# Seven quarter products for the first feed-forward layer's gate and up tiles, in five parts

## The chip, the cores and the metric

The kernel runs on one core of a Trainium2 chip. The metric is the device time of one execution in microseconds; less is better. TensorE (PE) multiplies, VectorE (DVE), ScalarE (ACT) and GpSimd (POOL) work element by element, and SyncE (SP) issues all transfers from the chip's main memory.

## The reference

Two blocks of two layers each work on 512 tokens of 1024 values: attention mixers with a modulation in the first block, a state-space mixer and a convolution module in the second. A gated feed-forward layer follows each mixer, four in all, with 2816 hidden values:

```
def _swiglu(h, wg, wu, wd):
    return (jax.nn.silu(h @ wg) * (h @ wu)) @ wd
...
    cond = jax.nn.silu(c)
    for l in range(DEPTH):
        mod = cond @ ada_w[l] + ada_b[l]
        sh1, sc1, g1, sh2, sc2, g2 = [m[:, None, :] for m in jnp.split(mod, 6, axis=-1)]
...
        h = _rms_norm(x, norm_ffn[l]) * (1.0 + sc2) + sh2
        x = x + g2 * _swiglu(h, ffn_gate[l], ffn_up[l], ffn_down[l])
```

`mod` is a product of one vector with a 1024 x 6144 matrix for each layer of the first block: 48 columns of 128 values per layer.

## The kernel before

**Precision by splitting.** Each float32 operand becomes a high part `hi` (a rounded copy, made by ACT, L297) and a low part `lo` (the rest, made by DVE, L298); a product is three matmuls, hi by hi, hi by lo and lo by hi (`mm3`, L305 to L307). So every weight tile that lands in `raw` (three buffers) costs an ACT copy and a DVE subtraction before PE can use it. The split tiles have four buffers each.

**A feed-forward layer** (`ffn`) has 22 hidden tiles of 128 values. Its program alternates between *gate and up tiles* (`gu` or `gu7`, one per hidden tile, with result `d` as a hi and a lo part) and *down items* (`dn`, one per 128 output values, which multiply the `d` tiles of one part by `w_dn` and add into the stream `xT`, L675). `PARTS` says how many hidden tiles stand in a part.

- A **dense** tile (`gu`) needs 2 weight tiles x 8 row blocks x 3 = 48 matmuls of 512 columns, two splits on DVE, a product and the low part of `d`.
- A **seven** tile (`gu7`, `seven`) computes the same two products as a two by two block product from seven quarter products: 7 x 4 x 3 = 84 matmuls of 256 columns. DVE forms four sums of weights in `ws` (L710 to L714 here), splits three tiles of 1024 columns and one of 512, and joins the results (L740 and L816, L816 twice): 12 DVE instructions per tile in all with the low part of `d`. POOL adds two quarter results (L741). The sums of the activations (`crossed`, L687 to L693) are made once per layer.

Layer 0 (`ffn0`) computes all 22 tiles densely in three parts (`FIRST_S[0]` is 22); layers 1 to 3 compute 3, 2 and 2 tiles densely and the rest by seven products in four parts.

**The modulation stream.** Beside layer 0 runs `md.stream`: 56 columns of `ada` (8 of the first layer, 48 of the second) come in by transfers of 512 KB into `araw`, and each is reduced against `cb` by one DVE instruction of 1024 columns (L651, with an accumulator read), for a third of them followed by a small `gain` (L654). Two or three columns stand together, and `araw` has three buffers. `_weave` mixes the two streams by their costs in the order of the program text; a list scheduler then fixes the order on each engine. Every engine and SP's queue work strictly in that order, so an instruction that waits holds all behind it.

**Around layer 0.** The norm in front of it is made in halves of 256 tokens (`Split`): the first half of the dense tiles 0 and 1 runs while DVE builds the second half (L481, L492). The last two down items run as a `tail` in halves, so that the statistics of the next norm (`ss`, then `rb`) run under the second half's matmuls.

Of the kernel before, what the change touches and what calls it, by code (L numbers as in the profile page):

```python
# [10 lines left out]
F32 = mybir.dt.float32  # L11
F32R = mybir.dt.float32r
I32 = mybir.dt.int32
AF = mybir.ActivationFunctionType
OP = mybir.AluOpType
PSUM = bass.MemoryType.PSUM

T, NT, KC = 512, 4, 8
PARTS = ((0, 8), (8, 15), (15, 22))
PARTS_S = ((0, 6), (6, 12), (12, 17), (17, 22))  # L20
FIRST_S = (22, 3, 2, 2)
F_HID, FC = 2816, 22
NEG = -1e30

# [17 lines left out]
ROFF = {}  # L42
_o = 0
for _n, _w in ROW:
    ROFF[_n] = _o
    _o += _w
NROW = _o
CST = [("ident", 128), ("tri", 128), ("tri4", 128), ("cmask", 128), ("hones", 2)]
COFF = {}
_o = 0  # L50
# [40 lines left out]
def _layout(i):  # L91
# [20 lines left out]
    for n in range(4):  # L112
# [35 lines left out]
SSB = {"cbm": 2, "q": 16, "d": 14, "dt": 2, "xr": 1, "z": 2, "yg": 2, "xdt": 2, "L": 3, "xd": 1, "yo": 1, "sq": 1, "S": 1, "th": 1}  # L148
PHASES = {
# [9 lines left out]
    "ssm": (SSB,  # L159
# [63 lines left out]
def _program(nc, tc, a, out, stages=STAGES):  # L223
# [18 lines left out]
    def ptile(k, shape, dt, name):  # L242
        tag = ALIAS.get(name, name)
        _, p, bufs = cur[k]
        if k == "ps" and tag not in bufs:
            tag = {"tr": "pt", "st": "tr", "py": "tr"}[tag]
        return p.tile(shape, dt, tag=tag, name=name, bufs=bufs[tag])


# [1 line left out]

    xT = one.tile([128, KC, T], F32, name="xT")
    vec = one.tile([128, NVEC], F32, name="vec")
    row = one.tile([128, NROW], F32, name="row")
    cst = one.tile([128, NCST], F32, name="cst")
    ones = one.tile([128, 128], F32, name="ones")
    X = [xT[:, c] for c in range(KC)]
# [11 lines left out]
    def cs_(name, n):  # L269
        return cst[:, COFF[name]:COFF[name] + n]  # L270

    def rw(name, n):
        return row[:, ROFF[name]:ROFF[name] + n]

    ident = cs_("ident", 128)
    tri = cs_("tri", 128)
# [1 line left out]
    def tmp(name="t", dt=F32, n=T):  # L278
        return ptile("sb", [128, n], dt, name)
# [348 lines left out]
    class Mod:  # L628
# [25 lines left out]
                V.scalar_tensor_tensor(self.gain[:, o + c:o + c + 1], col, self.nb[:, o + c:o + c + 1],  # L654
                                       vc(nm, 8 * self.l + c), op0=OP.add, op1=OP.mult)

        def pair(self, j):
            for i in range(2):
                self.column(j, i)

        def stream(self, r):
            for j in r:
                self.pair(j)
                yield 1.0

        def col(self, o):
            return lambda c: self.mod[:, o + c:o + c + 1]
# [74 lines left out]
        return s, r1, bu[:, :hv]  # L742

    def ffn(n, nm, gcol, nxt):
        sparse = FIRST_S[n] < FC
        direct = isinstance(nm, Split)
        phase(("ffn1" if direct else "ffn") if sparse else "ffn0")
        x4 = []
        h = nm.h

# [14 lines left out]
        def gu(js):  # L765
            def it():
                gr = []
                for j in js:
                    with tc.issue_after(nm.mark.ins) if direct and j == 1 else nullcontext():
                        W = direct and j == 0 and nm.W or two(a[f"w_gu{n}"][j])  # L770
                        gr += [(psum("pg"), W[0]), (psum("pu"), W[1])]
                if js[0] == 0 and direct:
                    if sparse:
                        nm.keep = [tmp("z") for c in range(KC)]
                        for z, (hi, lo) in zip(nm.keep, h):
                            o = HALVES[0]
                            G.tensor_tensor(z[:, o], hi[:, o].bitcast(F32), lo[:, o].bitcast(F32), op=OP.add)
                    nm.lin([gr[:2], gr[2:]])
                else:
                    lin(gr, h)  # L780
                if sparse and len(x4) < 4:
                    sums(range(4) if direct else range(2 * js[0], 2 * js[0] + 2))
                if nm.R is None:
                    nm.finish().to_sbuf()
                R = nm.R
                for i, j in enumerate(js):
                    pg, pu = gr[2 * i][0], gr[2 * i + 1][0]
                    s = tmp("s")
                    if direct:
                        S.activation(s, pg, AF.Silu)  # L790
                        V.tensor_tensor(s, s, pu, op=OP.mult)
                    else:
                        u = tmp("su")
                        V.tensor_tensor(s, pg, R, op=OP.mult)
                        S.activation(s, s, AF.Silu)
                        V.tensor_tensor(u, pu, R, op=OP.mult)
                        V.tensor_tensor(s, s, u, op=OP.mult)
                    d[j] = hilo_of(s, to="d")
                return 10.4 * len(js), None
            return it  # L800
# [24 lines left out]
            return item(a[f"w_dn{n}"][m][:, lo:hi], lambda: [d[j] for j in range(lo, hi)], ev, hi - lo)  # L825

        items = []
        for lo, hi in (PARTS_S if sparse else PARTS):
            b = lo
            if lo == 0 and direct:  # L830
                items.append(gu([0, 1]))
                b = 2
            items += [gu([j]) if j < FIRST_S[n] else gu7(j) for j in range(b, hi)]
            at = TAIL_AT["final" if isinstance(nxt, Final) else 7]
            n_tail = at[0] if hi == FC and isinstance(nxt, Split) else 0
            items += [dn(m, lo, hi) for m in range(KC - n_tail)]
            if n_tail:
                items.append(tail(range(KC - n_tail, KC), lambda m: a[f"w_dn{n}"][m][:, lo:hi], hi - lo,
                                  lambda: [d[j] for j in range(lo, hi)], gcol, nxt, ("pj",) * n_tail, at[1:]))
# [132 lines left out]
    def mix0(make, following):  # L972
# [29 lines left out]
        for c in range(KC):  # L1002
# [9 lines left out]
                o = slice(j * 128, (j + 1) * 128)  # L1012
                mm3(pi[j], wh[:, 0, o], wl[:, 0, o], xh, xl, c == 0, c == KC - 1)
            mm3(pw[:72], wh[:, 0, 640:], wl[:, 0, 640:], xh, xl, c == 0, c == KC - 1)
        nc.sync.dma_start(row, a["row"].to_broadcast([128, NROW]))
        iq = {}
        B = {}
        for dst, key, i in ((iq, 4, 0), (B, 0, 1)):
# [16 lines left out]
        prod = small(64, "lp", bufs=1)  # L1035
        ls = small(2, "ls", bufs=1)
        for i in range(2):
            V.tensor_tensor_reduce(prod, rw(f"lam_q{i + 1}", 64), rw(f"lam_k{i + 1}", 64), 1.0, 0.0,
                                   OP.mult, OP.add, accum_out=ls[:, i:i + 1])
        with tc.issue_after(mk.ins):  # L1040
            S.activation(ls, ls, AF.Exp)
# [181 lines left out]
    def mix1(nm, md, nx):  # L1223
# [56 lines left out]
        def f3(u, pT):  # L1280
            i, t = u
            kv = ODD_Q[i] // 4
            p0 = 64 * (kv % 2)
            t0 = max(t - 1, 0)
            if t == 0:
                pys[i] = psum("py")
            o = slice(t * 64, t * 64 + 64)
            for s in range(t0, t + 1):
                c0 = s * 128 + p0
                E.matmul(pys[i][:, o], pT[:, (s - t0) * 128:(s - t0 + 1) * 128], Vn[kv // 2][:, c0:c0 + 64],  # L1290
                         start=(s == t0), stop=(s == t))
            if t == NT - 1:
                e = small(4, "es", bufs=2)
                S.activation(e, nms[i], AF.Exp, bias=row[:, ROFF["sinks"] + i:ROFF["sinks"] + i + 1])
                V.tensor_tensor(rs[i], rs[i], e, op=OP.add)
                head_out(i, pys.pop(i), rs[i], y, 0)

# [483 lines left out]
    if stages[0] != "mix0":  # L1781
        phase("ffn0")
        consts()
        nc.sync.dma_start(row, a["row"].to_broadcast([128, NROW]))
        if stages[0] in STAGES[:4]:
            cond()
            mods()
# [45 lines left out]
```

## Time and profile before

| what | value |
|---|---|
| time, median of 3 runs (lowest to highest) | 2675.92 us (2673.03 to 2680.61) |
| the profiled execution: its own time, its span | 2680.65 us, 2678.9 us |
| PE, DVE, ACT, POOL busy, share of the span | 94%, 73%, 47%, 21% |
| mean granted clock of PE | 0.972 |

Layer 0's products stand at about 373 to 744 us of the span, those of layer 1 at about 949 to 1316 us.

### The profile page before, as it was taken

The page shows a single profiled execution, that of the slowest core. Times are in us where ns is not written, and L with a number is a line of the kernel's source. Part 1 is how long each engine was busy: PE and PEld are TensorE (multiplying, and loading weights), DVE is VectorE, ACT ScalarE, POOL GpSimd, SP SyncE. Part 2 cuts the span into 40 slices and gives each one's busy share as a digit, 9 for nine tenths or more (in the row PEclk, how much of TensorE's full clock was granted, in tenths as well). Part 3 has the DMA queues.
Part 4 walks back from the last instruction along what each step waited for, and adds up shares of the span by engine and source line. Part 5 has one row for each costly group of instructions (what it writes and reads, how often), then busy time and mean ns, then how long its engine had stood idle before and what let it go on. Part 6 is the DMA issues. An engine that isn't in the chain of part 4 may idle for free.

```text
span 2678.9 us, 39465 instructions
## 1 busy us (share of the span) xinstructions
PE 2519.2 (94%) x15104; PEld 2222.2 (83%) x15104; DVE 1951.8 (73%) x3448; ACT 1255.4 (47%) x2291; POOL 557.1 (21%) x383
## 2 busy tenths in 40 slices
PE   5787989999999989999999999999999996999998
PEld 3666888888888879999788888789999786799997
DVE  7898755555456676677678887778777798678776
ACT  4456642222357543544455544454445554545443
POOL 3344220000112250000100000131012684321102
PEclk9889999999999999999999999999999997999999
DMA  7711025555421113333322121223333110132332
GB/s 259 240 56 40 32 87 204 173 176 193 149 73 40 40 56 102 95 104 104 103 79 72 45 89 56 87 81 103 108 104 106 69 63 16 64 117 94 102 98 87
DMA packets 84733, 265.75 MB, mean 99 GB/s; under 512 B 9280, under 2 KB 11712, under 8 KB 84544
## 3 DMA queue, kind: packets, MB, share of 16 engines
q1 hardware_dynamic: 84544, 263.24, 29.4%
q8 instruction: 118, 1.93, 0.3%
q14 instruction: 71, 0.58, 0.1%
HBM read 261.10 MB, written 2.10 MB: 98 GB/s over the span
## 4 chain that ended last, share of the span: by engine, by line
PE 71%; DVE 15%; issue 4%; POOL 3%; DMA 3%; ACT 3%; DVEq 0%; SPq 0%; POOLq 0%; ACTq 0%
PE pj L305 10%; PE pj L306 10%; PE pj L307 10%; PE pg L305 5%; PE pg L307 5%; PE pg L306 5%; PE pu L307 4%; PE pu L305 4%; PE pu L306 4%; DVE lo L298 3%; DMA raw<-w_gu 2%; POOL yp L1600 1%; PE pj L1412 1%; PE pj L1413 1%; PE pj L1414 1%
## 5 line engine op out<-in xcount | busy, mean ns | idle before, releaser
L297 ACT CAST hi<-raw 128x1024 fp32r<-128x1024 f32 (+5 forms) x445 | 393.5, 893 | 687.7 <-PE pj L306 265.9
L298 DVE TENSOR_TENSOR lo<-raw,hi 128x1024 fp32r<-128x1024 f32 (+5 forms) x435 | 465.7, 1073 | 170.7 <-ACT hi L297 167.9
L305 PE MATMUL pj<-d,hi 128*128 128x512 f32 (+1 forms) x940 | 353.3, 384 | 3.5 <-DVE xT L679 1.7
L306 PE MATMUL pj<-d,hi 128*128 128x512 f32 (+1 forms) x940 | 353.9, 379 | 0.0
L307 PE MATMUL pj<-d,lo 128*128 128x512 f32 (+1 forms) x940 | 351.0, 379 | 0.0
L741 POOL TENSOR_TENSOR bu<-bu 128x256 f32<-128x256 f32 x59 | 110.7, 1876 | 774.1 <-ACT bu L737 760.5
L305 PE MATMUL pu<-hi 128*128 128x256 f32 (+1 forms) x736 | 230.1, 314 | 3.2 <-DVE z L481 3.2
L307 PE MATMUL pu<-hi,lo 128*128 128x256 f32 (+1 forms) x736 | 231.1, 314 | 0.2 <-DVE lo L298 0.2
L306 PE MATMUL pu<-lo,hi 128*128 128x256 f32 (+1 forms) x736 | 229.8, 313 | 0.0
L305 PE MATMUL pj<-hi 128*128 128x512 f32 (+2 forms) x520 | 208.7, 405 | 3.9 <-ACT qk L901 1.2
L306 PE MATMUL pj<-lo,hi 128*128 128x512 f32 (+2 forms) x520 | 208.8, 402 | 3.6 <-DVE lo L492 2.4
L305 PEld LDWEIGHTS pj<-d,hi 128*128 128x128 f32 x940 | 177.2, 189 | 37.8 <-DVE xT L679 2.3
L307 PE MATMUL pj<-hi,lo 128*128 128x512 f32 (+2 forms) x520 | 206.5, 398 | 0.3 <-DVE lo L298 0.3
L306 PEld LDWEIGHTS pj<-d,hi 128*128 128x128 f32 x940 | 177.9, 189 | 33.2 <-issue 1.0
L307 PEld LDWEIGHTS pj<-d,lo 128*128 128x128 f32 x940 | 177.6, 189 | 33.3 <-issue 0.5
L305 PE MATMUL pg<-xh,hi 128*128 128x256 f32 x708 | 199.1, 281 | 1.2 <-ACT ua L734 1.1
L305 PE MATMUL pg<-hi 128*128 128x256 f32 (+1 forms) x572 | 192.2, 336 | 7.1 <-DVE z L481 4.5
L307 PE MATMUL pg<-xh,lo 128*128 128x256 f32 x708 | 198.1, 280 | 0.0
L306 PE MATMUL pg<-xl,hi 128*128 128x256 f32 x708 | 198.0, 280 | 0.0
L307 PE MATMUL pg<-hi,lo 128*128 128x256 f32 (+1 forms) x572 | 191.9, 335 | 4.6 <-DVE lo L298 4.5
L306 PE MATMUL pg<-lo,hi 128*128 128x256 f32 (+1 forms) x572 | 191.3, 335 | 0.6 <-DVE lo L492 0.6
L297 ACT CAST hi<-ws 128x1024 fp32r<-128x1024 f32 x118 | 123.5, 1049 | 116.3 <-DVE ws L711 50.7
(474 smaller groups left out, 6360.6 us busy)
## 6 DMA issues: line engine op xcount, KB each, us to landing
raw<-w_gu SPq DMA_DIRECT2D x176, 512.0 KB, 3.7
araw<-ada SPq DMA_DIRECT2D x96, 512.0 KB, 5.9
raw<-w_dn SPq DMA_DIRECT2D x48, 384.0 KB, 3.1
raw<-w_dn SPq DMA_DIRECT2D x48, 320.0 KB, 2.9
raw<-w_p SPq DMA_DIRECT2D x24, 512.0 KB, 3.6
raw<-w_out SPq DMA_DIRECT2D x32, 256.0 KB, 2.8
raw<-w_xs SPq DMA_DIRECT2D x16, 512.0 KB, 3.4
raw<-w_z SPq DMA_DIRECT2D x16, 512.0 KB, 3.4
```

The lines of the kernel that those rows point to most:

```text
L297: S.copy(hi, raw)
L298: (eng or V).tensor_tensor(lo, raw, hi.bitcast(F32), op=OP.subtract)
L305: E.matmul(ps, lh, rh, start=start, stop=False, **k)
L306: E.matmul(ps, lh, rl, start=False, stop=False, **k)
L307: E.matmul(ps, ll, rh, start=False, stop=stop, **k)
L741: G.tensor_tensor(bu[:, :hv], bu[:, :hv], bu[:, hv:], op=OP.add)
L1412: E.matmul(o, xh[:, ts], wh[:, k], start=st_, stop=False, skip_group_check=True)
L1413: E.matmul(o, xh[:, ts], wl[:, k], start=False, stop=False, skip_group_check=True)
L1414: E.matmul(o, xl[:, ts], wh[:, k], start=False, stop=sp, skip_group_check=True)
L1600: G.tensor_tensor(yp[:, sft:], yp[:, sft:], pr[:, sft:], op=OP.add)
```

## The change

Layer 0 takes the path of layer 1: tiles 0 to 2 stay dense, tiles 3 to 21 are made by seven products, and its parts are of 5, 5, 4, 4 and 4 tiles instead of 8, 7 and 7. Its buffers are set anew: `araw` two instead of three, `d` ten halves instead of sixteen, and the buffers of the seven products are added; squares share the tag `z`. The modulation stream is woven in by single columns instead of pairs. Four rows of constants that only the first mixer reads (`lam`) leave the lasting tile `row` for a tile of that stage, with a transfer of their own.

```diff
-PARTS = ((0, 8), (8, 15), (15, 22))
-PARTS_S = ((0, 6), (6, 12), (12, 17), (17, 22))
-FIRST_S = (22, 3, 2, 2)
+PARTS = (((0, 5), (5, 10), (10, 14), (14, 18), (18, 22)),) + (((0, 6), (6, 12), (12, 17), (17, 22)),) * 3
+FIRST_S = (3, 3, 2, 2)
...
-    "ffn0": ({"araw": 6, "cb": 2, "d": 16, "z": 3, "su": 2, "sq": 2}, {"mm": 6, "st": 1, "tr": 1}),
+    "ffn0": ({"araw": 4, "cb": 2, "d": 10, "z": 8, "ws": 3, "xh": 4, "xl": 4, "ua": 2, "bu": 2}, {"mm": 6, "st": 1, "tr": 1}),
...
-    row = one.tile([128, NROW], F32, name="row")
+    row = one.tile([128, NROW - NLAM], F32, name="row")
...
         def stream(self, r):
             for j in r:
-                self.pair(j)
-                yield 1.0
+                for i in range(2):
+                    self.column(j, i)
+                    yield 0.5
...
-        sparse = FIRST_S[n] < FC
         direct = isinstance(nm, Split)
-        phase(("ffn1" if direct else "ffn") if sparse else "ffn0")
+        phase("ffn" if n > 1 else f"ffn{n}")
...
-        for lo, hi in (PARTS_S if sparse else PARTS):
+        for lo, hi in PARTS[n]:
...
-        nc.sync.dma_start(row, a["row"].to_broadcast([128, NROW]))
+        rows()
+        lam = ptile("sb", [128, NLAM], F32, "lam")
+        nc.sync.dma_start(lam, a["row"][:, :NLAM].to_broadcast([128, NLAM]))
```

In the changed file lines stand about four further down (L298 is L302, L651 is L655, L675 is L676).

The first place is DVE's queue where layer 0 begins, behind the second half of the norm. Before, the columns of the stream (L651) stand there, then the splits of dense tile 2's two weights (L298):

```order
L651 ISA araw,mod_95<-araw,cb,vec 128x1024
L651 ISA mod_95 128x1
L492 SCALAR_TENSOR_TENSOR lo<-z,mod_95,hi 128x256
L651 ISA araw,mod_95<-araw,cb,vec 128x1024
L651 ISA mod_95 128x1
L651 ISA araw,mod_95<-araw,cb,vec 128x1024
L651 ISA mod_95 128x1
L651 ISA araw,mod_95<-araw,cb,vec 128x1024
L651 ISA mod_95 128x1
L298 TENSOR_TENSOR lo<-raw,hi 128x1024
```

Now four of the norm's low parts (L496) follow two columns, and the sums of the activations (L690, L691, L694) stand between the other columns, all ahead of the split of tile 2 (L302):

```order
L655 ISA araw,mod_95<-araw,cb,vec 128x1024
L655 ISA mod_95 128x1
L691 SCALAR_TENSOR_TENSOR ws<-ws,z 128x256 x2
L690 SCALAR_TENSOR_TENSOR ws<-z,ws 128x256
L655 ISA araw,mod_95<-araw,cb,vec 128x1024
L655 ISA mod_95 128x1
L691 SCALAR_TENSOR_TENSOR ws<-ws,z 128x256
L694 TENSOR_TENSOR xl<-ws,xh 128x1024
L655 ISA araw,mod_95<-araw,cb,vec 128x1024
L655 ISA mod_95 128x1
L302 TENSOR_TENSOR lo<-raw,hi 128x1024
```

So six columns stand ahead of tile 2's split as before, and seven instructions for the sums of the activations have come between.

The second place is DVE's queue in the middle of a run of gate and up tiles. Before, one dense tile there takes this much, two columns included:

```order
L298 TENSOR_TENSOR lo<-raw,hi 128x1024
L791 TENSOR_TENSOR s<-s,pu 128x512
L298 TENSOR_TENSOR lo<-raw,hi 128x1024
L390 TENSOR_TENSOR d<-s,d 128x512
L651 ISA araw,mod_100<-araw,cb,vec 128x1024
L651 ISA mod_100 128x1
L651 ISA araw,mod_100<-araw,cb,vec 128x1024
L651 ISA mod_100 128x1
```

Now most of a seven tile of the second part takes this much (from the third sum of weights `ws` on), one column and its `gain` (L658) included:

```order
L712 TENSOR_TENSOR ws<-ws,raw 128x512
L741 TENSOR_TENSOR s<-pu,ua 128x512
L655 ISA araw,mod_100<-araw,cb,vec 128x1024
L655 ISA mod_100 128x1
L658 SCALAR_TENSOR_TENSOR gain_101<-mod_100,nb_102,vec 128x1
L714 TENSOR_TENSOR ws<-ws,raw 128x512
L302 TENSOR_TENSOR lo<-ws,hi 128x1024
L815 SCALAR_TENSOR_TENSOR s<-s,bu 128x256
L815 SCALAR_TENSOR_TENSOR s<-s,pg 128x256
L302 TENSOR_TENSOR lo<-ws,hi 128x1024
L302 TENSOR_TENSOR lo<-raw,hi 128x512
L302 TENSOR_TENSOR lo<-raw,hi 128x1024
```

Two more sums (L711, L715) and the low part of `d` (L394) belong to a tile as well: four instructions of a dense tile have become twelve, and from tile to tile one or two columns stand between them.

The third place is SP's queue and DVE's where the second part goes over into its down items. SP issues, behind the last `w_gu` loads, those of `w_dn` two at a time with one column's transfer behind each pair, and goes on so to the end of the section:

```order
L709 DMA raw<-w_gu 128x1024 x2
L645 DMA araw<-ada 128x1024 x2
L295 DMA raw<-w_dn 128x640 x2
L645 DMA araw<-ada 128x1024
L295 DMA raw<-w_dn 128x640 x2
```

DVE takes two columns there, ahead of the low part of the part's last `d` (L394) and of the adds into `xT` (L676):

```order
L655 ISA araw,mod_100<-araw,cb,vec 128x1024
L655 ISA mod_100 128x1
L302 TENSOR_TENSOR lo<-raw,hi 128x640
L815 SCALAR_TENSOR_TENSOR s<-s,bu 128x256
L815 SCALAR_TENSOR_TENSOR s<-s,pg 128x256
L302 TENSOR_TENSOR lo<-raw,hi 128x640
L655 ISA araw,mod_100<-araw,cb,vec 128x1024
L655 ISA mod_100 128x1
L394 TENSOR_TENSOR d<-s,d 128x512
L676 SCALAR_TENSOR_TENSOR xT<-pj,mod_95,xT 128x512 x2
```

Before, pairs of columns stood behind such loads; now single ones do, and a load can be issued only when the DVE instruction that empties its buffer is done.

## Rows read from the trace of the kernel before

**Rows 1.** Windows: us, PE, PEld, DVE, ACT, POOL busy, clock, DMA, GB/s.

```profile
373.00:411.00 38.00, 35.70 (x236) 33.46 (x237) 28.99 (x53) 15.93 (x27) 5.49 (x6) 0.91 0.58 202
411.00:744.00 333.00, 331.52 (x1499) 274.89 (x1498) 178.02 (x257) 88.95 (x112) 9.67 (x8) 1.00 0.51 171
949.00:996.00 47.00, 40.19 (x273) 37.25 (x272) 42.47 (x62) 26.39 (x48) 29.26 (x28) 0.96 0.17 56
996.00:1316.00 320.00, 316.42 (x2134) 292.38 (x2133) 224.97 (x299) 149.23 (x238) 32.19 (x25) 0.99 0.32 102
```

**Rows 2.** ACT in order of time: first reads of dense and seven tiles' results.

```profile
637.53 0.59 ACT L790 ACTIVATE s<-pg 128x512 f32<-128x512 f32 x1
702.75 0.59 ACT L790 ACTIVATE s<-pg 128x512 f32<-128x512 f32 x1
...
1072.24 0.37 ACT L737 COPY bu<-pg 128x256 f32<-128x256 f32 x1
1092.22 0.37 ACT L737 COPY bu<-pg 128x256 f32<-128x256 f32 x1
```

**Rows 3.** Windows of four seven tiles of layer 1, their sum and mean.

```profile
sum 39.98, PE 39.98 PEld 39.94 DVE 34.01 ACT 24.18 POOL 4.50; mean PE 9.99 PEld 9.98 DVE 8.50 ACT 6.05 POOL 1.12
```

**Rows 4.** DVE's groups by form, 411 to 744 us: busy us, mean ns, idle before.

```profile
L651 DVE CUSTOM_DVE_ANT_0 araw<-araw,cb,vec 128x1024 f32<-128x1024 f32 x33 | 42.0, 1283 | 34.0 <-DMA araw<-ada 34.0
L651 DVE CUSTOM_DVE_ANT_0 araw<-araw,cb 128x1024 f32<-128x1024 f32 x16 | 19.6, 1225 | 49.9 <-DMA araw<-ada 49.8
L675 DVE SCALAR_TENSOR_TENSOR xT<-pj,mod,xT 128x512 f32<-128x512 f32 x22 | 16.5, 748 | 25.7 <-PE pj L307 25.7
L654 DVE SCALAR_TENSOR_TENSOR gain<-mod,nb,vec 128x1 f32<-128x1 f32 x16 | 3.5, 218 | 0.3
```

**Rows 5.** DVE's group that layer 1's stretch, 996 to 1316 us, holds for its successor.

```profile
L384 DVE SCALAR_TENSOR_TENSOR lo<-xT,vec,hi 128x512 fp32r<-128x512 f32 x8 | 9.2, 1181 | 0.2 <-ACT hi L383 0.2
```

**Rows 6.** DVE's waits, 411 to 744 us: us in total, times, longest.

```profile
DVE araw L651 <- DMA araw<-ada: 83.8, 24, 5.7
DVE lo L298 <- ACT hi L297: 38.6, 13, 7.3
```

**Rows 7.** DVE's waits in layer 1's steady stretch, 996 to 1316 us.

```profile
DVE lo L298 <- ACT hi L297: 35.2, 27, 4.7
DVE ws L710 <- DMA raw<-w_gu: 21.4, 14, 2.6
```

**Rows 8.** Landing of `araw` in 360 to 744 us, then of `w_gu` in 996 to 1316 us.

```profile
DMA to landing us min/median/max: 3.7/6.1/9.3
...
DMA to landing us min/median/max: 3.0/3.9/5.9
```

**Rows 9.** DVE in order of time where layer 0 begins.

```profile
390.11 1.75 DVE L651 CUSTOM_DVE_ANT_0 araw<-araw,cb,vec 128x1024 f32<-128x1024 f32 x1
391.80 0.08 DVE L651 DVE_READ_ACCUMULATOR2_ANT mod<- 128x1 f32 x1
...
397.42 1.29 DVE L651 CUSTOM_DVE_ANT_0 araw<-araw,cb,vec 128x1024 f32<-128x1024 f32 x1 [2.12 <-DMA araw<-ada]
...
399.89 1.22 DVE L298 TENSOR_TENSOR lo<-raw,hi 128x1024 fp32r<-128x1024 f32 x1
```

**Rows 10.** PE's wait for tile 2's split in layer 0's start.

```profile
PE pg L307 <- DVE lo L298: 1.9, 1, 1.9
```

**Rows 11.** DVE in order of time: a sum of activations in layer 1's start.

```profile
973.13 0.96 DVE L689 SCALAR_TENSOR_TENSOR ws<-z,ws 128x256 f32<-128x256 f32 x1
```

**Rows 12.** DVE and POOL groups by form, 1077.63 to 1107.99 us: joining a seven tile.

```profile
L741 POOL TENSOR_TENSOR bu<-bu 128x256 f32<-128x256 f32 x3 | 2.2, 742 | 25.0 <-ACT bu L737 25.0
...
L816 DVE SCALAR_TENSOR_TENSOR s<-s,bu 128x256 f32<-128x256 f32 x3 | 1.3, 417 | 0.0
```

**Rows 13.** The chain of waits at layer 0's end: start, us, what.

```profile
736.42 0.13 PE pj L307
...
738.49 0.61 PE ss L462 x4
...
742.61 0.43 PE rb L471 x2
```

More of the change, by code (lines that the diff above doesn't have):

```diff
@@ L47 @@
 NROW = _o
+NLAM = ROFF["sinks"]
 CST = [("ident", 128), ("tri", 128), ("tri4", 128), ("cmask", 128), ("hones", 2)]
@@ L244, in ptile @@
         _, p, bufs = cur[k]
-        if k == "ps" and tag not in bufs:
-            tag = {"tr": "pt", "st": "tr", "py": "tr"}[tag]
+        if tag not in bufs:
+            tag = {"tr": "pt", "st": "tr", "py": "tr", "sq": "z"}[tag]
         return p.tile(shape, dt, tag=tag, name=name, bufs=bufs[tag])
@@ L270, in cs_, with rw, rows @@
         return cst[:, COFF[name]:COFF[name] + n]
-    def rw(name, n):
-        return row[:, ROFF[name]:ROFF[name] + n]
+    def rw(name, n, o=0):
+        o += ROFF[name] - NLAM
+        return row[:, o:o + n]
+    def rows():
+        nc.sync.dma_start(row, a["row"][:, NLAM:].to_broadcast([128, NROW - NLAM]))
     ident = cs_("ident", 128)
@@ L655, in column @@
                                        vc(nm, 8 * self.l + c), op0=OP.add, op1=OP.mult)
-        def pair(self, j):
-            for i in range(2):
-                self.column(j, i)
         def stream(self, r):
             for j in r:
-                self.pair(j)
-                yield 1.0
+                for i in range(2):
+                    self.column(j, i)
+                    yield 0.5
         def col(self, o):
@@ L772, in it @@
                 if js[0] == 0 and direct:
[L773 to L777, printed above, removed]
+                    nm.keep = [tmp("z") for c in range(KC)]
+                    for z, (hi, lo) in zip(nm.keep, h):
+                        o = HALVES[0]
+                        G.tensor_tensor(z[:, o], hi[:, o].bitcast(F32), lo[:, o].bitcast(F32), op=OP.add)
                     nm.lin([gr[:2], gr[2:]])
@@ L780, in it @@
                     lin(gr, h)
-                if sparse and len(x4) < 4:
+                if len(x4) < 4:
                     sums(range(4) if direct else range(2 * js[0], 2 * js[0] + 2))
@@ L1037, in mix0 @@
         for i in range(2):
-            V.tensor_tensor_reduce(prod, rw(f"lam_q{i + 1}", 64), rw(f"lam_k{i + 1}", 64), 1.0, 0.0,
+            V.tensor_tensor_reduce(prod, lam[:, 128 * i:128 * i + 64], lam[:, 128 * i + 64:128 * i + 128], 1.0, 0.0,
                                    OP.mult, OP.add, accum_out=ls[:, i:i + 1])
@@ L1293, in f3 @@
                 e = small(4, "es", bufs=2)
-                S.activation(e, nms[i], AF.Exp, bias=row[:, ROFF["sinks"] + i:ROFF["sinks"] + i + 1])
+                S.activation(e, nms[i], AF.Exp, bias=rw("sinks", 1, i))
                 V.tensor_tensor(rs[i], rs[i], e, op=OP.add)
@@ L1783, in _program @@
         consts()
-        nc.sync.dma_start(row, a["row"].to_broadcast([128, NROW]))
+        rows()
         if stages[0] in STAGES[:4]:
```

2 rows, old and new, of the table PHASES are left out of this document.

## The prediction

> **What bounds the kernel now.** I read the windows by stage first. Between 411 and 744 us, layer 0's steady stretch from tile 3 on, PE is busy 331.5 of 333 us at full clock and DVE only 178 [rows 1]: the stage is bound by the number of matmul columns. DVE's waits there look large, 83.8 us for columns of the modulation and 38.6 us for ACT's high parts [rows 6], and cost nothing: DVE has far more time than work, and PE's busy time shows that no product waited for it. Layer 1 shows the form that layer 0 is to take. Its stretch from 996 to 1316 us does the same 19 hidden tiles with 320 us, PE 316 and DVE 225 [rows 1]. In the middle of its runs of gate and up tiles PE is busy all the time and DVE 8.50 of 9.99 us [rows 3]. So the seven products move a stage from "PE alone" to "PE, with DVE at 85%", and layer 1 has no modulation stream on DVE. The question is whether the columns still fit.
>
> **What the change saves on PE.** ACT's first reads of the results give the rhythm of the tiles: six dense tiles from 637.53 to 702.75, 10.87 us each; two seven tiles from 1072.24 to 1092.22, 9.99 us each [rows 2]. 0.88 us over 19 tiles is 16.7 us, if nothing else stops PE. The two stretches themselves differ by 333 - 320 = 13 us [rows 1]. Down items keep their number of columns; there are five sections of eight instead of three.
>
> **What it puts on DVE.** Layer 1's stretch holds 225 us of DVE work, of which 9.2 us belong to the layer after it [rows 5]: 215.8. The columns that now come beside it: 49 of them, 42.0 + 19.6 us, and 3.5 us for their gains [rows 4], 65.1 us. The fifth part means eight more adds into the stream than layer 1 has, at 0.75 us [rows 4], 6.0 us. Together 287 us. Against today's 333 us that leaves 46 us, against layer 1's 320 us 33 us. Work alone does not make DVE the bound; work and waits may. In a queue worked in order every wait is time that DVE does not get back unless PE has products in stock, and 33 us over 19 tiles is 1.7 us a tile.
>
> **What DVE will wait for.** A column can be taken when its 512 KB have landed, 6.1 us in the median after the issue, 3.7 at least [rows 8]; and it can be issued when the buffer is free and SP's queue has come to it. With two `araw` buffers a transfer is issued at the earliest when the column two before it is done. I went through the new order and added up, with the durations of these rows, the DVE work that stands between the instruction that releases the transfer and the column. In the runs of gate and up tiles it is 6 to 9 us: landing is covered. The loads of `w_gu` have 3.7 to 4.8 us of work against a landing of 3.9 [rows 8]: some 5 us of waits in all (layer 1 shows 21.4 us of them [rows 7], where DVE arrives early). In the down sections 15 columns have only 0.6 to 4.9 us, together 40.8, since each transfer stands in SP's queue behind two loads of `w_dn`, the second of which needs a buffer that a split has just emptied. The second column of the third place in the order shows it: the first split of 640 columns there empties the buffer, and up to the column stand two joins of 0.42 us [rows 12] and one split of 640 columns, less than the 1.22 of a whole one [rows 9]: under 2.1 us of work for a landing of some 5. Queued behind that column is the low part of the part's last `d`, which the down items need. At the median landing the 15 waits come to 15 x 6.1 - 40.8 = 51 us, at the shortest to 15 x 3.7 - 40.8 = 15. The loads of a down section are smaller than those of a gate and up run, which speaks for less than the median; I take the middle, 4.9 us, 33 us. DVE then needs 287 + 33 + 5 = 325 us for a stretch in which PE needs 316: DVE becomes the bound by a little, and the stretch takes 325 instead of 333, **-8 us**. The bounds: -16.7 (all waits fall where PE has products in stock), +10 (51 us of waits).
>
> **The start.** Six columns stand ahead of tile 2's split as before, and between them now seven instructions for the sums of the activations. Six of these cost 0.96 us beside POOL [rows 11] (0.42 where POOL is still [rows 12]) and one is as long as a split, 1.22 [rows 9]: 7.0 us. PE already waits 1.9 us for this split today [rows 10], so what makes it later lies on the path. Against it stands a wait of 2.12 us for a column [rows 9] that the sums fill: +4.9, I take **+5**. Bounds: +1.6 (sums at 0.42: 3.7 - 2.1); +13.1 (one whole landing of 6.1 more, since the third column has two buffers instead of three, and nothing is filled). Layer 1's start, which has these sums but no columns, is 47 us long against 38 here [rows 1]: 9 us more, between my value and the upper bound, but its lead-in differs, so I leave it as evidence for the bound.
>
> **The end.** The last two down items run in halves, so that the statistics `ss` pass under the second half; the first half's last product ends at 736.5, `ss` comes at 738.49 and `rb` at 742.61 [rows 13], 4.1 us of chain. With four `d` tiles in the last part instead of seven the second half has 2 x 3 x 3 matmuls fewer, at 0.13 us each [rows 13] 2.3 us of cover less. I take **+1.5** (0 to 2.3).
>
> **The rest.** The transfer of `lam` and the renamed buffers touch nothing that waits: 0. POOL's additions (19 of 0.742 us [rows 12]) are in layer 1's DVE time already; the columns that meet them are dearer: a column beside POOL took 1.75 us instead of 1.29 [rows 9]. An addition and a column together take 2.0 us, 19 times in 320 us: 12% or 6 of the 49 columns would meet one, at 0.46 us 2.7 us, which I leave inside the bounds of the waits. The Trainium skill, "SBUF — State Buffer", section "Who interferes with whom", says that DVE with two inputs in SBUF and GpSimd reading SBUF exclude each other for the whole instruction; the 1.75 us agrees with that. By it each POOL addition could hold DVE for its whole length, which is the third rival below.
>
> **Sum.** -8 + 5 + 1.5 = -1.5 us against the profiled execution's own 2680.65 us (span 2678.9, 1.75 around it). That execution is 4.7 us above the median; I put the difference on the median: 2675.92 - 1.5 = **2674.4 us**. A measurement of this kernel can tell 0.3%, 8 us, from no change.
>
> **Rivals.**
> - *DVE keeps pace, faster.* The scheduler lets matmuls of down items run between the products of the part's last tiles, so PE has work while DVE waits for a column, and DVE's waits of 122 us today [rows 6] cost PE nothing. Then the stretch gains the whole 16.7, the start costs 3, the end 1: 2663.2. Against it: every down item needs a split by DVE that stands behind the same columns, and DVE's stock of time is 33 us now, not 155. Chance 0.30.
> - *The column waits become the bound, slower.* Every one of the 15 columns in the down sections waits a median landing: 51 us, DVE 343, +10 + 5 + 1.5 = +16.5: 2692.4. It decides from 42.5 us of waits for columns on: DVE is then at 287 + 5 + 42.5 = 334.5, +1.5, and with 6.5 for start and end the loss is 8 us. For it: the landing of 6.1 us is that of today's stretch, at 171 GB/s [rows 1]; against it: the shorter loads. Chance 0.22.
> - *POOL holds DVE.* Were all 19 additions to hold a column for their whole 0.742 us, DVE has 325 + 14.1 = 339: +6 + 6.5 = +12.6, 2688.5. The one row that shows it cost 0.46, not 0.74, and the additions seldom meet a column. Chance 0.06.
>
> That the products are not removed at all cannot be: the order shows them gone.
>
> **From the cases to the numbers.** The forecast has 0.42 and a range of its own of 2665 to 2684 (landings from 4.3 to 5.5 us move the waits by 9). The first rival lies beyond -8 us, and so do some of the forecast's short landings: faster 0.33. The second and third lie beyond +8, and some of the forecast: slower 0.29; same 0.38. The range goes from a little below the first rival, 2660, to a little above the second, 2694.
>
> **What would show it.** In the windows of the new stretch (about 411 to 738): PE busy about 316 with some 9 us idle in four places, one at the head of each down section, and DVE above 280. DVE's waits for `araw` there near 33 us, nearly all in the down sections; under 20 speaks for the first rival, about 50 for the second. Tile 2's split done at about 406 instead of 401.1 [rows 9]. ACT's first reads 10 us apart in the middle of the runs; 10.9 would mean that DVE binds everywhere and that the sum of its work is wrong, not its waits. Between `ss` and `rb` PE idle by 1 to 2 us. The forecast falls if PE is idle mainly inside the runs of gate and up tiles, if the start loses over 10 us, or if the difference comes from another stage.

## The result, and the profile after

| | before | changed |
|---|---|---|
| median of 4 runs, us | 2678.27 | 2695.24 |
| lowest to highest | 2673.03 to 2681.32 | 2694.58 to 2700.74 |
| ratio, 95% interval | | 1.0077 (1.0061 to 1.0093) |
| span of the profiled execution | 2678.9 | 2692.8 |

The kernel is slower by 17 us between the medians, 0.77% by the ratio. The forecast of 2674.4 was wrong, and the result lies 1.2 us above its range. From the page of the changed kernel, how long each engine is busy (us, share of the span, number of instructions):

```profile
PE 2516.2 (93%) x15770; PEld 2245.8 (83%) x15770; DVE 2074.2 (77%) x3641; ACT 1315.9 (49%) x2428; POOL 601.1 (22%) x420
```

Four marks on PE divide layer 0: its second `rb` (382.6 us before, 375.2 now), the end of tile 2 before (413.5) and the first product with a sum of activations now (414.1), the first `ss` of the end (738.5, 750.8) and the last `rb` (757.7, 769.8). I call what lies between them start, stretch and end. The second mark is not quite the same place in the two kernels. In the changed one the last matmul of tile 2 (512 columns) begins at 411.16 and ends at 411.5, and matmuls of tile 3 (256 columns) follow:

```profile
411.16 0.39 PE L311 MATMUL pu<-hi,lo 128*128 128x512 f32 x1
411.38 0.28 PE L310 MATMUL pg<-lo,hi 128*128 128x256 f32 x1
```

So its start holds 2.6 us of tile 3's products. Windows of the kernel before for start and stretch (us; PE, PEld, DVE, ACT, POOL busy; granted clock; DMA share; GB/s):

```profile
382.60:413.50 30.90, 29.05 (x185) 26.35 (x184) 24.85 (x38) 13.92 (x23) 3.43 (x4) 0.94 0.62 221
413.50:738.50 325.00, 324.46 (x1453) 268.58 (x1452) 171.98 (x237) 86.70 (x108) 8.95 (x7) 1.00 0.51 172
```

The same of the changed kernel:

```profile
375.20:414.10 38.90, 33.80 (x206) 30.50 (x207) 38.36 (x50) 19.86 (x33) 19.33 (x14) 0.91 0.35 116
414.10:750.80 336.70, 316.81 (x2114) 291.16 (x2113) 278.07 (x418) 142.45 (x237) 32.06 (x26) 0.98 0.52 173
```

The start is 8.0 us longer (5.4 up to the end of tile 2), the stretch 11.7, the end as long as it was (19.0 against 19.2). In the profiled execution the program ahead of layer 0 was 7.4 us shorter and what follows 1.8 longer: 13.9 us in the span. How much of the 7.4 us is scatter is open: in the other profiles of kernels with the changed layout the second `rb` stands anywhere from 376.2 to 382.6. Layer 0 itself lost 19.5 us, between the 17 of the medians and the 20.6 of the ratio.

In the stretch PE is idle for 336.7 - 316.8 = 19.9 us, and before for 0.5. What it waits for, and what DVE waits for, from 411 to 744 us:

```profile
DVE araw L655 <- DMA araw<-ada: 23.3, 9, 5.0
DVE lo L302 <- ACT hi L301: 16.0, 20, 2.0
DVE xT L676 <- PE pj L311: 6.5, 4, 3.2
DVE ws L711 <- DMA raw<-w_gu: 3.6, 5, 2.0
...
PE pu L311 <- DVE lo L302: 11.1, 10, 1.9
```

DVE's waits for columns went from 83.8 us [rows 6] to 23.3, fewer than the 33 of the forecast; yet PE now waits for DVE. Windows of single sections show where: a run of five seven tiles (460 to 512), a down section (581 to 609) and a run of four tiles; behind them four short windows, to which I come below:

```profile
460.40:511.90 51.50, 46.82 (x386) 45.99 (x385) 50.42 (x77) 27.68 (x46) 4.42 (x4) 1.00 0.48 168
581.10:609.10 28.00, 26.80 (x135) 22.14 (x134) 18.77 (x31) 6.99 (x12) 0.87 (x1) 1.00 0.58 191
609.10:651.10 42.00, 39.12 (x302) 38.51 (x301) 38.93 (x61) 21.57 (x36) 3.34 (x3) 0.92 0.48 161
...
465.60:472.00 6.40, 6.37 (x53) 6.37 (x54) 5.96 (x8) 2.53 (x7) 0.00 (x0) 1.00 0.91 317
615.30:621.30 6.00, 5.97 (x28) 5.98 (x29) 5.71 (x8) 2.48 (x5) 0.00 (x0) 0.50 0.75 254
686.20:689.60 3.40, 3.40 (x18) 3.40 (x17) 3.40 (x5) 0.74 (x2) 0.00 (x0) 0.50 0.84 306
747.60:750.80 3.20, 2.68 (x12) 2.68 (x13) 0.86 (x4) 0.81 (x2) 1.46 (x2) 0.50 0.26 99
```

In the run of five DVE is busy 50.42 of 51.50 us, 98%, and in the run of four 38.93 of 42.00, 93%; in the down section 18.77 of 28.00, 67%. My 287 us of work against 333 was a mean over two regimes. ACT's first reads of the tiles' results show the rhythm of the tiles in these two runs:

```profile
471.86 0.38 ACT L738 COPY bu<-pg 128x256 f32<-128x256 f32 x1 [2.95 <-PE pg L311]
483.00 0.38 ACT L738 COPY bu<-pg 128x256 f32<-128x256 f32 x1 [2.96 <-PE pg L311]
492.98 0.38 ACT L738 COPY bu<-pg 128x256 f32<-128x256 f32 x1 [2.96 <-PE pg L311]
504.59 0.38 ACT L738 COPY bu<-pg 128x256 f32<-128x256 f32 x1 [2.95 <-PE pg L311]
...
623.98 0.38 ACT L738 COPY bu<-pg 128x256 f32<-128x256 f32 x1 [3.60 <-PE pg L311]
633.96 0.38 ACT L738 COPY bu<-pg 128x256 f32<-128x256 f32 x1 [2.96 <-PE pg L311]
643.95 0.38 ACT L738 COPY bu<-pg 128x256 f32<-128x256 f32 x1 [2.96 <-PE pg L311]
```

In the run of five the tiles come 11.1, 10.0 and 11.6 us apart; in the run of four 10.0, as in layer 1, and so in the runs on either side of it. There PE loses its time at the first tile of the run, just behind the down section, and at the last. Added up from PE's single waits, the 19.9 us of idle time are 7.5 at the first tiles of runs, 2.3 between tiles (in the run of five alone), 2.5 at last tiles, 3.1 in the down sections and 4.5 at the end.

The head of the run at 609 us shows how a first tile loses time, DVE in order of time, then PE's two waits:

```profile
609.04 1.23 DVE L655 CUSTOM_DVE_ANT_0 araw<-araw,cb 128x1024 f32<-128x1024 f32 x1
610.19 0.08 DVE L655 DVE_READ_ACCUMULATOR2_ANT mod<- 128x1 f32 x1
610.19 0.75 DVE L676 SCALAR_TENSOR_TENSOR xT<-pj,mod,xT 128x512 f32<-128x512 f32 x1
610.86 0.68 DVE L712 TENSOR_TENSOR ws<-ws,raw 128x512 f32<-128x512 f32 x1
611.45 1.28 DVE L655 CUSTOM_DVE_ANT_0 araw<-araw,cb,vec 128x1024 f32<-128x1024 f32 x1
...
614.05 1.22 DVE L302 TENSOR_TENSOR lo<-ws,hi 128x1024 fp32r<-128x1024 f32 x1
...
612.75 0.38 PE L309 MATMUL pu<-xh,hi 128*128 128x256 f32 x1 [0.65 <-ACT hi L301]
...
615.33 0.58 PE L311 MATMUL pu<-xh,lo 128*128 128x256 f32 x1 [1.80 <-DVE lo L302]
```

Two columns and the adds of the down section before stand in DVE's queue between the sums of weights of the first tile; the low part that PE needs comes out at 615.3, 1.80 us late. Behind that wait the granted clock is 0.50 from 615.3 to 621.3, the lower of the two levels (1.2 GHz), at which 28 matmuls of 256 columns take 6.0 us, 0.21 each, where the run goes at 9.99 / 84 = 0.12. So this wait of 1.8 us costs some 2.6 us more. Not every such wait does: the short windows above show the clock at 0.50 behind another wait of 1.80 us (at 684.7) from 686.2 to 689.6 and around one of 4.53 us (at 748.1), but at 1.00 behind one of 1.89 us (at 465.6).

### The profile page after: what moved, and what is told of

It is laid out like the page before. It is cut to its first block, busy times and chain, and to the rows that moved or that the text cites. A ratio compares the mean times of both kernels' runs of the same rounds, so it can differ in the third digit from the quotient of the medians.

```text
span 2692.8 us, 41333 instructions
## 1 busy us (share of the span) xinstructions
PE 2516.2 (93%) x15770; PEld 2245.8 (83%) x15770; DVE 2074.2 (77%) x3641; ACT 1315.9 (49%) x2428; POOL 601.1 (22%) x420
## 4 chain that ended last, share of the span: by engine, by line
PE 63%; DVE 20%; DMA 6%; issue 5%; ACT 3%; POOL 3%; SPq 0%; DVEq 0%; POOLq 0%; ACTq 0%
PE pj L309 9%; PE pj L310 8%; PE pj L311 8%; PE pg L311 4%; PE pg L309 4%; PE pg L310 4%; DVE lo L302 4%; DMA raw<-w_gu 4%; PE pu L311 3%; PE pu L310 3%; PE pu L309 3%; DMA araw<-ada 2%; DVE araw L655 2%; POOL yp L1601 2%; PE pj L1413 1%
## 5 line engine op out<-in xcount | busy, mean ns | idle before, releaser
L301 ACT CAST hi<-raw 128x1024 fp32r<-128x1024 f32 (+4 forms) x460 | 386.0, 852 | 543.7 <-PE pj L310 209.2
L302 DVE TENSOR_TENSOR lo<-raw,hi 128x1024 fp32r<-128x1024 f32 (+4 forms) x450 | 458.1, 1023 | 149.2 <-ACT hi L301 145.3
L742 POOL TENSOR_TENSOR bu<-bu 128x256 f32<-128x256 f32 x78 | 130.1, 1668 | 1070.3 <-ACT bu L738 1010.0
L309 PE MATMUL pg<-xh,hi 128*128 128x256 f32 x936 | 264.4, 282 | 2.1 <-ACT ua L735 1.1
L311 PE MATMUL pg<-xh,lo 128*128 128x256 f32 x936 | 262.7, 281 | 0.0
L310 PE MATMUL pg<-xl,hi 128*128 128x256 f32 x936 | 262.5, 280 | 0.0
L301 ACT CAST hi<-ws 128x1024 fp32r<-128x1024 f32 x156 | 163.3, 1049 | 143.8 <-DVE ws L712 71.6
L302 DVE TENSOR_TENSOR lo<-ws,hi 128x1024 fp32r<-128x1024 f32 x156 | 196.5, 1264 | 19.8 <-ACT hi L301 19.5
L311 PEld LDWEIGHTS pj<-d,lo 128*128 128x128 f32 x934 | 176.5, 189 | 35.4 <-DVE lo L302 3.0
L309 PEld LDWEIGHTS pg<-xh,hi 128*128 128x128 f32 x936 | 177.7, 190 | 5.0 <-ACT ua L735 1.9
L310 PEld LDWEIGHTS pg<-xl,hi 128*128 128x128 f32 x936 | 177.3, 189 | 1.5
```

Source lines behind the costliest of these rows:

```text
L301: S.copy(hi, raw)
L302: (eng or V).tensor_tensor(lo, raw, hi.bitcast(F32), op=OP.subtract)
L309: E.matmul(ps, lh, rh, start=start, stop=False, **k)
L310: E.matmul(ps, lh, rl, start=False, stop=False, **k)
L311: E.matmul(ps, ll, rh, start=False, stop=stop, **k)
L742: G.tensor_tensor(bu[:, :hv], bu[:, :hv], bu[:, hv:], op=OP.add)
```

## The experiments

What the kernels gave, from windows between the marks (the medians of the kernel before beside them were 2675.4 us for 1 to 4, 2677.1 for 5 to 8 and 2677.7 for 9 to 12; for the kernels with tile 3 dense, tile 2's end ends the start, which in the others would be 2.2 to 2.7 us shorter by that mark, 4.1 in the second; "idle" is the stretch less PE's busy time):

| kernel | median us, ratio to before (95%) | start | stretch | PE busy, idle in it |
|---|---|---|---|---|
| before | 2678.3 | 30.9 | 325.0 | 324.5, 0.5 |
| changed | 2695.2, 1.0077 | 38.9 | 336.7 | 316.8, 19.9 |
| 1 short reduction | 2686.5, 1.0044 (1.0028 to 1.0059) | 35.7 | 327.7 | 313.0, 14.7 |
| 2 short transfer | 2689.3, 1.0052 (1.0036 to 1.0068) | 35.4 | 330.1 | 315.3, 14.8 |
| 3 both short | 2676.4, 1.0008 (0.9992 to 1.0025) | 33.2 | 317.7 | 308.6, 9.1 |
| 4 columns to down items | 2698.0, 1.0093 (1.0068 to 1.0117) | 39.1 | 337.3 | 316.2, 21.1 |
| 5 dense, five parts | 2687.9, 1.0038 (1.0024 to 1.0053) | 37.8 | 331.9 | 327.9, 4.0 |
| 6 lam rows alone | 2679.9, 1.0010 (0.9998 to 1.0022) | | | |
| 7 columns on POOL | 2763.5, 1.0330 (1.0314 to 1.0345) | | | |
| 8 last eight tiles seven | 2693.6, 1.0058 (1.0040 to 1.0075) | 36.5 | 336.2 | 325.9, 10.3 |
| 9 fewer columns in the start | 2702.1, 1.0088 (1.0072 to 1.0104) | 34.1 | 345.6 | 319.5, 26.2 |
| 10 end mended | 2705.5, 1.0099 (1.0082 to 1.0115) | 39.1 | 342.9 | 319.4, 23.6 |
| 11 start and end | 2708.0, 1.0116 (1.0101 to 1.0131) | 33.9 | 349.8 | 321.7, 28.1 |
| 12 both mended, both short | 2669.4, 0.9962 (0.9951 to 0.9974) | 32.2 | 316.3 | 309.2, 7.1 |

**1 to 3: which cost of a column is it?** Theory A is DVE's work in the runs, theory B the waits for landing. `beside[0]` is set for the stream beside layer 0 alone. The first edit is that of the second and third kernel, the other that of the first and third; the second reduces seven copies of the 128 elements instead.

```diff
+            w = 128 if beside[0] else 1024
-            nc.sync.dma_start(r, a["ada"][self.l, j][:, i])
+            nc.sync.dma_start(r[:, :w], a["ada"][self.l, j][:, i][:, :w])
...
+                v = 128 if beside[0] else 1024
-                V.tensor_tensor_reduce(r, r, cbx[0], 1.0, 0.0 if gain else b, OP.mult, OP.add, accum_out=col)
+                V.tensor_tensor_reduce(r[:, :v], r[:, :v], cbx[0][:, :v], 1.0, 0.0 if gain else b, OP.mult, OP.add, accum_out=col)
```

> The columns beside layer 0 are reduced over 128 of their 1024 elements, so their values are not those of the reference; their transfers stay whole. DVE spends about 0.25 us on a column instead of 1.3, on 49 columns some 50 us less. Theory A, DVE's work in the runs of gate and up tiles is what binds (1.8 columns a tile on top of 8.5 us of a 9.99 us tile): the 12 us of PE's waits there and the 5 us of half clock behind them go, about 2680 us. Theory B, the waits for the landing of columns bind: the transfers are as before, so 2691 to 2699 us.

> The columns beside layer 0 come by transfers of 128 instead of 1024 elements per partition, and DVE reduces seven copies of these, 896 elements, so it works nearly as long as before (about 1.1 us) and the values are not those of the reference. Theory A: DVE's work is almost unchanged, so about 2690 us, at most 5 us below the changed kernel. Theory B: the 23 us of waits for araw go and with them most of the loss, 2675 to 2683 us.

> Both at once: transfers of 128 elements and reductions over 128, values not those of the reference. Both theories: the layer runs at PE's speed, stretch near 308 us instead of 337; what is left of the loss then comes from the start and the end: 2665 to 2672 us. Theory A sees the first experiment close to this one, theory B the second.

Neither theory holds alone: the first kernel's 2686.5 us lie between the two, the second's 2689.3 are theory A's, and the third's 2676.4 lie above what both gave. Against the changed kernel the stretch is 9.0 us shorter with short work, 6.6 with short transfers, 19.0 with both. That both give more than the two together (15.6) comes from one profile of each; by the ratios the gains are 8.8, 6.7 and 18.5 us, each uncertain by some 5 us, so it is not shown. The waits for columns of the first kernel, then of the second (411 to 744 us):

```profile
DVE araw L657 <- DMA araw<-ada: 39.1, 21, 5.1
```

```profile
DVE araw L659 <- DMA araw<-ada: 20.0, 11, 4.0
```

With 38 us less of work in that window (DVE is busy 238.93 us of it instead of 276.75) DVE, in the first kernel, waits 39.1 instead of 23.3 us for columns: it comes to them earlier and stands in its queue all the same, with the splits behind it. The two costs lie in one queue, and what the work gives up the waits partly take. In the second kernel the waits have hardly gone, though a transfer lands after 3.2 us in the median instead of 5.1. So it does not test theory B as it was meant to, and where its 6.6 us come from is open: DVE's waits for high parts fell from 16.0 to 12.0 us, and the traffic in the stretch from 173 to 109 GB/s. The third kernel shows what the seven products are worth, the stretch's window:

```profile
412.20:729.90 317.70, 308.58 (x2114) 285.44 (x2112) 235.30 (x419) 144.77 (x238) 31.54 (x26) 1.00 0.37 112
```

PE needs 308.6 us for the same 2114 matmuls at full clock, 15.9 less than before (about 1 us of it, an estimate, is work on the other side of a mark: 24 matmuls of 256 columns, 0.12 us each, stand in the start, and 18 of 512, 0.23 each, have come in from the end for 18 of 256). In the changed kernel they take 316.8, 8.2 us more. In its three places at 0.50 PE is busy 12.0 us, so 6.0 of these 8.2 us are lower clock; what the other 2.2 are is not shown.

**4: more columns with the down items.** A wrapper gives each item of layer 0 a cost of its own for the weave:

```diff
+        def cost(c, it):
+            def f():
+                k, post = it()
+                return (c if n == 0 else k), post
+            return f
...
-            items += [dn(m, lo, hi) for m in range(KC - n_tail)]
+            items += [cost(0.75, dn(m, lo, hi)) for m in range(KC - n_tail)]
```

(1.0 for a seven tile, 6 for tiles 0 to 2, 3 for the last four items, 56.5 in all instead of 345.)

> The weave's costs in layer 0 are set to 1.0 for a seven tile and 0.75 for a down item, so that about one column stands with each seven tile and three with each four down items. Theory A: DVE has 18.8 us of work in 28 us of a down section and 98 % in a gate and up run, so moving work there gains 8 to 15 us: 2680 to 2687 us. Theory B: more columns where the landing is not covered, so more waits: 2695 to 2705 us.

Nothing gained: 2698.0 us, in theory B's range, stretch 337.3. The loads are issued ahead of their use, so in DVE's order most of the moved columns stand ahead of the low part of a run's last `d`, and DVE waits 26.8 us for columns from 411 to 744 us instead of 23.3. The experiment did not bring columns into the idle time of the down sections, and so does not decide what that would give.

**5 and 6: the rest of the change without seven products.** The fifth sets `FIRST_S[0]` to 22 in the changed kernel (the sums of the activations are still formed in the start, without use); the sixth takes only the hunks on `lam` and `row` into the kernel before.

> The changed kernel with all 22 tiles of layer 0 dense again: five parts, two araw buffers, single columns and the moved lam rows stay. If the loss comes from the columns beside seven tiles, nothing is left of it: the stretch from the second rb to the first ss of the tail stays within 3 us of the 355.9 of the kernel before, and the time is 2668 to 2680 us. If the five parts, the two buffers or the single columns cost something by themselves, it shows here: above 2685 us. The first mixer ends some 4 to 8 us earlier than before if the lam rows do that.

> The kernel before with only the four lam rows moved to their own tile and transfer. If the earlier first rb of layer 0 (359 to 363 us in five profiles against 367 before) is this edit's, the time is 2668 to 2672 us and rb stands at 359 to 363; if it is the scatter of a profile or comes with the new layer 0, the time is 2673 to 2678 us.

The lam rows do nothing that can be measured: the first `rb` stands at 366.2 us, and the 2679.9 us lie above both of the ranges. But the dense kernel with five parts is slower by 0.38%, the second case of its expectation, which neither theory had. So about half of the loss of 0.77% is there without one seven product, and whether the parts, the buffers, the single columns or the sums in the start bring it, this kernel does not separate. Its start is 6.9 us longer than before, its stretch too. The row of that:

```profile
418.50:750.40 331.90, 327.87 (x1451) 270.92 (x1450) 187.64 (x271) 89.02 (x124) 10.35 (x7) 0.99 0.51 170
```

DVE is busy 187.6 of 331.9 us here; 3.7 of PE's 4.0 us of idle time are one wait ahead of the second half of the last down items. The end of the changed kernel has the same wait, DVE in order of time, then PE:

```profile
744.08 1.38 DVE L302 TENSOR_TENSOR lo<-raw,hi 128x1024 fp32r<-128x1024 f32 x1 [1.55 <-ACT hi L301]
745.38 2.29 DVE L655 CUSTOM_DVE_ANT_0 araw<-araw,cb,vec 128x1024 f32<-128x1024 f32 x1
747.59 0.87 DVE L676 SCALAR_TENSOR_TENSOR xT<-pj,mod,xT 128x256 f32<-128x256 f32 x2
...
748.12 0.58 PE L309 MATMUL pj<-d,hi 128*128 128x256 f32 x1 [4.53 <-DVE xT L676]
```

PE waits 4.53 us for an add into the stream, which stands behind a split of the next stage's weights and a column that took 2.29 us beside POOL instead of 1.28. Items of four `d` tiles do not cover that.

**7: the columns on POOL.** `self.column(j, i)` gets `beside[0]` as its argument `on_pool`: POOL multiplies, ACT sums.

> The changed kernel with the columns beside layer 0 multiplied by POOL and summed by ACT, so that DVE takes neither their 1.3 us nor their waits. If both costs of the columns were DVE's alone, layer 0 runs like the third experiment: 2674 to 2684 us. If POOL's multiplications (about 3 us each by four times the 742 ns of 256 columns) hold DVE's instructions that read two operands, DVE loses up to 147 us: 2700 us and more.

2763.5 us, the second expectation. POOL's group and three of DVE's, 390 to 820 us:

```profile
L651 POOL TENSOR_TENSOR araw<-araw,cb 128x1024 f32<-128x1024 f32 x54 | 148.5, 2759 | 186.9 <-DMA araw<-ada 157.9 <-ACT hi L301 16.0 <-DVE ws L713 7.1
...
L302 DVE TENSOR_TENSOR lo<-raw,hi 128x512 fp32r<-128x512 f32 x41 | 47.1, 1150 | 11.8 <-ACT hi L301 11.5
...
L713 DVE TENSOR_TENSOR ws<-ws,raw 128x512 f32<-128x512 f32 x19 | 31.6, 1662 | 0.0
L677 DVE SCALAR_TENSOR_TENSOR xT<-pj,mod,xT 128x512 f32<-128x512 f32 x38 | 27.9, 744 | 12.9 <-PE pj L311 12.9
```

In the changed kernel the groups of DVE take 697, 744 and 746 ns (414 to 751 us). The adds into the stream, whose `pj` comes from PSUM, are not slowed; splits and sums with both operands in SBUF are, to 1150 and 1662. The Trainium skill, "SBUF — State Buffer", section "Who interferes with whom", states that a DVE instruction with two SBUF inputs contends with a GpSimd instruction that reads SBUF; the rows agree.

**8: seven products only where no columns stand.** `FIRST_S[0]` is 14; costs 4.0, 2.6 (dense), 0.02 (seven), 0.85 (down items of the first three parts), 0.02 behind.

> Tiles 0 to 13 of layer 0 dense, tiles 14 to 21 by seven products, and the weave's costs set so that nearly all columns stand beside the first three parts; the last two parts have none. Theories A and B alike: columns cost nothing beside dense tiles, seven tiles without columns run at 9.99 us, so 8 x 0.88 = 7 us are gained, less 2 us for the sums in the start and 3 us at the end: stretch 351 to 356 us, time 2670 to 2677 us. If columns also cost time beside dense tiles now that they stand closer (2.6 a tile), 2680 us and more.

2693.6 us: both theories missed, and the expectation's other case, above 2680, came true. The last two parts do run at about 10 us a tile, with waits of PE only at their first tile, but 36.5 us of start and 4.5 us of waiting at the end (744 us) remain, and single waits of 0.6 to 1.2 us now stand beside the dense tiles too.

**9 to 12: start and end mended.** The wrapper of the fourth experiment, with the old costs (10.4 a tile, 0.65 a row block) but 0.02 for tiles 0 and 1 in the ninth (total 324); in the tenth 0.02 for the last four items, total 318, and parts of 5, 4, 4, 4, 5; both in the eleventh (total 297); the twelfth adds the short transfer and reduction.

> The changed kernel with a weave that gives tiles 0 and 1 no columns, so that the six columns ahead of tile 2's split become two; the others stand a little closer behind. If the columns make the start long, the stretch from the second rb to the first seven product falls from 38.9 us to 33 to 35 and the time to 2686 to 2692 us. If the moved columns hold PE where they now stand, the time is 2692 to 2698 us.

> The changed kernel with parts of 5, 4, 4, 4 and 5 tiles and a weave in which the last columns stand with the last tiles, none with the last down items. If the short last part and the column there make PE wait 4.5 us ahead of the tail's second half, that wait falls to 2 us or less and the half clock behind it goes: 2687 to 2692 us. If the weights of the next stage make that wait, it stays and the time is 2693 to 2697 us.

> Both of the edits before. If places add up, 2680 to 2687 us; if DVE's work as a whole binds, so that a column moved only moves the wait, 2691 to 2697 us.

> The same with the columns beside layer 0 cut to 128 elements in transfer and reduction (values not those of the reference): what the seven products give where the columns cost next to nothing and start and end are mended. If the 16.7 us on PE are real, 2662 to 2669 us; if seven tiles lose that time by themselves (DVE's own work for the splits, the half clock behind short waits), 2672 to 2677 us as in the third experiment.

Each edit does at its place what it should, and the time rises past every range expected for the ninth, tenth and eleventh kernel. In the ninth the start falls from 38.9 to 34.1 us, and the stretch, with 52 columns instead of 49, grows by 8.9. In the tenth, whose parts differ too, the wait ahead of the end's second half falls from 4.53 to 1.1 us, and the stretch grows by 6.2, as the same columns stand closer: two with nearly every seven tile. This answers what the fourth left open in one direction: in both kernels, columns put closer beside seven tiles cost more. The twelfth kernel, at 0.9962 and a little above its first expectation, is the only one faster than before, and it is not the computation: with nearly free columns and a mended start and end the seven products give 8 us between medians (before was 2677.7 beside it). No version of the whole computation that beats the kernel before came out.

## Why the prediction was wrong, step by step

- *PE's saving, 16.7 us.* Near: 15.9 by PE's busy time in the third experiment, some 15 for the same work.
- *DVE's work, 287 us, and its waits, 38, against 333.* **This step failed, and it set the sign.** The terms that I had were near: 278 us of work, 23.3 us of waits for columns and 3.6 for `w_gu`. Two waits I had put at nothing without a reason, 16 us for ACT's high parts and 10 for PE's results; with them DVE comes to 331 us instead of 325, in a stretch of 336.7. And it was wrong to take the stretch for the larger of two sums: PE stood idle 19.9 us, 12.2 of them inside the runs, where my forecast had none and had named it as the sign that it falls. A seven tile leaves DVE 9.99 - 8.50 = 1.5 us; the order puts nine columns beside the five tiles from 460 to 512 us, 1.8 a tile, 1.33 us each (65.1 / 49): 8.50 + 2.4 = 10.9 us for 9.99. I had all these rows. Over 19 tiles that would be 17 us, an estimate; measured are the 12.2, since the shorter runs lose less (0.3 to 0.9 us a tile, and none at the first two seven tiles). What DVE has to spare in a down section does not help the next run: ahead of the run of five it waits there 5.0 us for a column, 2.0 for a high part and 2.0 for a load of `w_gu`, and still comes 1.9 us late.
- *What a wait of PE costs.* A step that was missing. I had priced only idle time; behind three of the four longest waits the granted clock is 0.50, and the same matmuls take 8.2 us more, 6.0 of them by the clock. So the stretch is -15.9 + 19.4 (idle) + 8.2 = +11.7 us, where the forecast had -8.
- *The start, +5.* It is +8.0 by the marks and +5.4 to the end of tile 2; the size was right, in part by luck. The split of tile 2 ends at 399.6 us, 24.4 after the second `rb`, where it was 401.1 [rows 9] and 18.5: 5.9 us later, near the 5; the wait of PE for it is 3.1 us instead of 1.9 [rows 10], and 1.3 us for a low part of the norm and 0.7 for a high part are new. DVE has no gap there, but some of its instructions are long; DVE, then POOL:

```profile
394.61 3.30 DVE L655 CUSTOM_DVE_ANT_0 araw<-araw,cb,vec 128x1024 f32<-128x1024 f32 x1
...
397.84 1.73 DVE L302 TENSOR_TENSOR lo<-raw,hi 128x1024 fp32r<-128x1024 f32 x1
...
393.48 3.35 POOL L694 TENSOR_TENSOR xl<-ws,xh 128x1024 fp32r<-128x1024 f32 x1 [3.66 <-ACT xh L693]
```

  Four columns took 1.75, one 3.30 (beside POOL's subtraction of 1024 columns) and the split 1.73 instead of 1.28 and 1.22: 4.4 us, where columns before were 0.8 us over. The seven sums themselves took 4.6 us and not 7.0. I counted POOL's hold on the sums and not on the six columns. The third rival had the mechanism, in the wrong place.
- *The end, +1.5 between `ss` and `rb`.* Misplaced: `rb` follows `ss` by 3.9 us instead of 4.1, with PE idle 1.7 of them instead of 0.9; what I had not seen is 4.5 us of waiting just ahead of `ss`, with half clock behind it, since the adds stand behind a column and the next stage's splits.
- *The lam rows, 0.* Right (1.0010).
- *The rivals.* The second gave 2692.4 us, close to the result by luck, by waits of 51 us for columns. They were 23.3. DVE was full (278 us of work and about 55 of waits in 337), but by more than those, and its fullness hurt in the runs, not in the down sections where I had put the waits: PE's waits for low parts `pu` in the runs are 11.1 us, those in the down sections some 3. The third is not in the stretch: a column there takes 1.31 or 1.26 us in the mean against 1.28 or 1.23 before [rows 4], 1.5 us for all 49.

What stays open: how the loss divides between the new layout (0.38% with dense tiles) and the columns beside seven tiles; how much of the 9 us of idle time that remains in the third experiment comes from DVE's own splits and how much from the loads; and whether columns truly placed into the idle time of the down sections would gain, since the fourth experiment did not place them there.

## What to carry to other kernels

When work is to be laid beside a faster stage, sum it for each regime of that stage, per tile, and not over the stage: 46 us to spare over 333 hid a tile that was 0.9 us too long. Price a short wait of the bounding engine with what follows it too: here each microsecond of idle time had about 0.3 us of lower clock behind it (6.0 for 19.9). And before a place is mended, ask whether the work moved away from it lands where it is scarcer: two local repairs that worked made the kernel slower.

## What the runs showed of the hardware that I had not expected

A column of 1024 elements on DVE, 1.28 us alone, took 3.30 us when it met one POOL subtraction of 1024 elements, which itself took 3.35; with POOL multiplying all columns, DVE's sums of 512 went from 744 to 1662 ns while its adds with an operand in PSUM stayed at 744. After a wait of 1.80 us PE's granted clock stood at 0.50 for the next 6.0 us, after another of 1.80 us for 3.4 us, and after one of 1.89 us it stayed at 1.00.
